# A residual RMSNorm on one core: a small first tile, pieces at the end, and a hardware loop of three tiles per iteration in between

## The chip, the cores and the metric

The kernel runs on 1 core of one Trainium2 chip. The metric is the device time of one execution in microseconds (us), as the median of several executions. All runs were fast (granted clock 1.0). The kernel before ran in every batch on the same chip as what it is compared with; its medians were 3736.6 to 3737.4 us. The batches ran on different chips, so a difference between kernels of two batches carries up to about 1 us of that.

Words used below: SP is the engine that issues all large transfers (DMA) here, DVE the vector engine, ACT the scalar engine. A transfer is *issued* when SP hands it to the DMA queue, *flows* while its packets move (16 side by side, on the core's 16 DMA engines), and has *landed* with the last of its landing records on its semaphore. Each of SP's transfers has 16 such records. A *slot* is a place in on-chip memory.

## The reference

```python
x, residual : 32 x 2048 x 2048 float32;  gamma : 2048 float32;  eps = 1e-6
z   = x + residual
rms = np.sqrt(np.mean(z ** 2, axis=-1, keepdims=True) + eps)
out = (z / rms * gamma).astype(np.float32)
```

That is 65536 rows of 2048 elements: two arrays read, one written, 1610.6 MB in all, and little arithmetic.

## The kernel before

The rows are cut into tiles of 6 x 128 rows (85 of them; a last tile of 2 x 128 is left over). A full tile is 6.29 MB. There are three slots for z, in turn, and one slot for the residual. The parts that matter:

```python
    R = 6
    NZ = 3
    sizes = [R] * n_full + ([left] if left else [])     # 85 full tiles, then one of 2
    ...
    def compute(i):
        # halves of 3 row blocks: DVE adds, ACT squares and sums, ACT takes the root
        ...
        # then DVE: reciprocal, and z * rstd * gamma, row block by row block
        ...

    load_x(0)
    load_r(0)
    load_gamma()
    load_x(1)
    compute(0)
    load_r(1)
    for i in range(1, n_tiles):          # written out by Python, 85 times
        store(i - 1)
        if i + 1 < n_tiles:
            load_x(i + 1)
        compute(i)
        if i + 1 < n_tiles:
            load_r(i + 1)
    store(n_tiles - 1)
```

Waits and semaphores are put in by the framework. In its built program every transfer counts up one of eight DMA semaphores, taken in rotation; in its trace the landing records lie on eight semaphores, 512 to 528 on each.

## Time and profile before

The median is 3736.8 us (3 runs, 3736.49 to 3737.15).

| what | value | how to read it |
|---|---|---|
| DMA queue | 99.7% of 16 engines' span | this is the bound |
| DVE, ACT busy | 62%, 29% | slack of over a third |
| flow in the middle | 433 GB/s | a tile in 43.6 us, three transfers of 14.5 us |
| all bytes at 433.3 GB/s | 3717 us | leaves about 19 us that are not flow |

From the page of the kernel before: busy time of DVE, the totals of the DMA, and the row of the main queue (packets, MB, share of 16 engines).

```profile
DVE 2311.6 (62%) x858; ACT 1078.6 (29%) x1197; POOL 0.2 (0%) x4
...
DMA packets 37180, 1610.83 MB, mean 431 GB/s; under 512 B 4132, under 2 KB 4132, under 8 KB 4132
...
q1 hardware_dynamic: 37152, 1610.63, 99.7%
```

Where are the 19 us? The view of stretches gives, for each stretch of time, its length, the busy time of DVE, ACT and POOL, the granted clock, the share of the DMA and the GB/s moved.

```profile
45.00:50.00 5.00, 3.69 (x3) 4.94 (x7) 0.00 (x0) 1.00 0.65 216
1800.00:1843.60 43.60, 27.04 (x10) 12.61 (x14) 0.00 (x0) 1.00 1.00 433
3690.00:3706.00 16.00, 15.96 (x6) 12.08 (x12) 0.00 (x0) 1.00 0.76 327
3706.00:3712.00 6.00, 5.96 (x5) 0.53 (x3) 0.00 (x0) 1.00 0.10 41
3712.00:3718.00 6.00, 6.00 (x2) 0.00 (x0) 0.00 (x0) 1.00 0.61 262
3718.00:3736.00 18.00, 5.32 (x4) 4.30 (x5) 0.00 (x0) 1.00 0.88 379
```

Two places are not full: one near 46 us, where the second residual load must wait for the adds of a whole first tile (13.1 us in SP's waits), and the last 46 us. In between the queue stays full, and the order of time shows why. This is one tile of the middle, in the kernel before: start, duration, engine (SPq is SP's issuing), line, operation, output and input.

```profile
1825.57 0.33 SPq L66 DMA_DIRECT2D r_slot<-in_residual_dram  x1
...
1839.65 0.34 SPq L69 DMA_DIRECT2D out_dram<-z  x1
1840.04 0.42 SPq L63 DMA_DIRECT2D z<-in_x_dram  x1
1856.11 6.56 DVE L76 TENSOR_TENSOR z<-z,r_slot 128x6144 f32<-128x6144 f32 x1 [16.49 <-DMA r_slot<-in_residual_dram]
```

The residual load is issued at 1825.57 and has landed at 1856.11, when DVE can add it. The store of the previous tile and the next x load go into the queue at 1839.65 and 1840.04, **16 us before that landing**. So when the residual has been moved, 29 us of work (two transfers of 14.5 us) stand behind it. While that backlog lasts, the wait for a landing and the next issue cost no flow (433 GB/s in this stretch). SP's own waits (total, times, longest) show how long it sits idle beside this:

```profile
SPq L66 <- DMA r_slot<-in_residual_dram: 1328.1, 85, 31.4
SPq L69 <- DVE z L98: 1183.3, 86, 20.1
SPq L66 <- DVE rstd L96: 1100.7, 83, 13.3
```

The stores (line 69) wait for DVE's last scaling, never for a residual load.

### The profile page before, as it was taken

What the parts mean: (1) busy time and instruction counts of PE and PEld (TensorE: products, weight loads), DVE (VectorE), ACT (ScalarE), POOL (GpSimd) and SP (SyncE); (2) the same over time, 40 slices, a digit from 0 to 9 for tenths busy, and PEclk for the clock granted to TensorE, in tenths of its full rate; (3) what the DMA queues carried; (4) which work ended last, traced back from release to release, by engine and by line L of the source; (5) the groups of instructions that cost most, each with busy time, mean ns of one, the idle gap of its engine ahead of it and who ended that gap; (6) DMA issues with size and microseconds to landing.
All of it is one profiled execution on the core that took longest, in us unless ns stands there. A gap on an engine that the chain in (4) does not pass through costs nothing.

```text
span 3736.0 us, 2707 instructions
## 1 busy us (share of the span) xinstructions
DVE 2311.6 (62%) x858; ACT 1078.6 (29%) x1197; POOL 0.2 (0%) x4
## 2 busy tenths in 40 slices
DVE  6555666665566666556666655666665566666556
ACT  2222233222223322222332222233222223322223
POOL 0000000000000000000000000000000000000000
DMA  9999999999999999999999999999999999999998
GB/s 410 429 432 434 433 434 432 435 433 434 433 434 433 433 434 434 433 435 432 434 433 434 434 434 433 434 432 435 432 436 432 435 432 435 433 434 433 435 432 369
DMA packets 37180, 1610.83 MB, mean 431 GB/s; under 512 B 4132, under 2 KB 4132, under 8 KB 4132
## 3 DMA queue, kind: packets, MB, share of 16 engines
q1 hardware_dynamic: 37152, 1610.63, 99.7%
q14 instruction: 20, 0.16, 0.0%
q10 hardware_dynamic: 8, 0.03, 0.0%
HBM read 1073.77 MB, written 536.87 MB: 431 GB/s over the span
## 4 chain that ended last, share of the span: by engine, by line
DMA 70%; DVE 30%; issue 0%; ACT 0%; DVEq 0%; SPq 0%
DMA r_slot<-in_residual_dram 70%; DVE z L76 30%; DVE z L98 0%; ACT sq_junk L79 0%; DVE rstd L96 0%; DVEq L160 0%; DVEq L76 0%; SPq L63 0%; ACT rms L86 0%
## 5 line engine op out<-in xcount | busy, mean ns | idle before, releaser
L76 DVE TENSOR_TENSOR z<-z,r_slot 128x6144 f32<-128x6144 f32 x171 | 1111.7, 6542 | 1385.4 <-DMA r_slot<-in_residual_dram 1385.4
L79 ACT ACTIVATE sq_junk<-z 128x2048 f32<-128x2048 f32 x512 | 963.5, 1882 | 2620.0 <-DVE z L76 2603.5
L98 DVE SCALAR_TENSOR_TENSOR z<-z,rstd,gamma_tile 128x2048 f32<-128x2048 f32 x512 | 1173.6, 2347 | 6.0
L79 ACT ACTIVATION_READ_ACCUMULATOR sq_junk<-z 128x1 f32 x512 | 95.5, 186 | 0.0
L86 ACT ACTIVATE rms<-ssq,eps_tile 128x3 f32<-128x3 f32 x171 | 50.7, 296 | 5.5
L96 DVE RECIPROCAL rstd<-rms 128x3 f32<-128x3 f32 x171 | 29.5, 172 | 5.7 <-ACT rms L86 5.7
L114 DVE LOAD_MASK_SELECT gamma_tile<-gamma_tile x1 | 0.0, 14 | 17.8 <-DMA gamma_tile<-in_gamma_dram 17.8
L79 ACT ACT_TABLE_LOAD x1 | 1.3, 1283 | 18.8 <-DMA z<-in_x_dram 18.8
L114 DVE STREAM_SHUFFLE gamma_tile<-gamma_tile 128x2048 f32<-128x2048 f32 x1 | 2.4, 2418 | 0.0
L109 DVE MEMSET gamma_tile<- 128x2048 f32 x1 | 1.8, 1765 | 0.4 <-issue 0.4
L86 ACT ACT_TABLE_LOAD x1 | 1.3, 1283 | 0.0
L60 DVE MEMSET eps_tile<- 128x1 f32 x1 | 0.1, 59 | 0.8 <-PEq L146 0.8
L146 POOL MEMSET const-bfloat16-1.0<- 128x1 bf16 x1 | 0.1, 101 | 0.0
L146 POOL MEMSET const-uint8-127<- 128x1 uint8 x1 | 0.1, 101 | 0.0
L146 POOL MEMSET const-float32-0.0<- 128x1 f32 x1 | 0.1, 98 | 0.2 <-issue 0.2
L146 POOL MEMSET const-float32-1.0<- 128x1 f32 x1 | 0.1, 98 | 0.0
## 6 DMA issues: line engine op xcount, KB each, us to landing
z<-in_x_dram SPq DMA_DIRECT2D x85, 6144.0 KB, 45.0
r_slot<-in_residual_dram SPq DMA_DIRECT2D x85, 6144.0 KB, 30.4
out_dram<-z SPq DMA_DIRECT2D x85, 6144.0 KB, 30.9
z<-in_x_dram SPq DMA_DIRECT2D x1, 2048.0 KB
r_slot<-in_residual_dram SPq DMA_DIRECT2D x1, 2048.0 KB
out_dram<-z SPq DMA_DIRECT2D x1, 2048.0 KB, 7.3
gamma_tile<-in_gamma_dram ACTq DMA_DIRECT2D x4, 8.0 KB
```

The costliest lines, as they stand in the source:

```text
L60: nc.vector.memset(eps_tile, float(eps))
L76: nc.vector.tensor_add(out=z[:, a:b, :], in0=z[:, a:b, :], in1=r_slot[:, a:b, :])
L79: nc.scalar.activation(out=sq_junk, in_=z[:, g, :], func=Act.Square, accum_out=ssq[:, g - a : g - a + 1],)
L86: nc.scalar.activation(out=rms[:, : b - a], in_=ssq[:, : b - a], func=Act.Sqrt, bias=eps_tile, scale=inv_d,)
L96: nc.vector.reciprocal(out=rstd[:, : b - a], in_=rms[:, : b - a])
L98: nc.vector.scalar_tensor_tensor(out=z[:, g, :], in0=z[:, g, :], scalar=rstd[:, g - a : g - a + 1], in1=gamma_tile, op0=mult, op1=mult,)
L109: nc.vector.memset(gamma_tile, 0.0)
L114: nc.vector.stream_shuffle(gamma_tile, gamma_tile, [0] * 32)
L146: nc = _bacc.Bacc("TRN2", target_bir_lowering=False, num_devices=1)
```

## The change

The intent: take away the idle queue at both ends, and shrink the program. The left-over tile of 2 x 128 rows comes first, its residual goes into a z slot that is still free, so that both first and both second loads are issued at once. The last tile, now a full one, is loaded, computed and stored in pieces of two row blocks. The 81 tiles 2 to 82 run in a hardware loop: 27 iterations of three tiles (so that the slots come round), with addresses taken from registers. Its semaphores are not reset at the back edge (its trace has a clear of semaphores only at the end, at line 221); instead the waits compare them with registers that grow each iteration.

```diff
-    sizes = [R] * n_full + ([left] if left else [])
+    sizes = ([left] if left else []) + [R] * n_full
...
+    def pieces(i):
+        k = sizes[i]
+        return [(a, min(a + piece, k)) for a in range(0, k, piece)] if i == last else [(0, k)]
+
+    def r_of(i):
+        return z_slots[NZ - 1] if i == 0 else r_slot
...
+    def cycle(i, at):
+        z_next = z_slots[(i + 1) % NZ]
+        nc.sync.dma_start(out=o_full[at - 1], in_=z_slots[(i - 1) % NZ])
+        nc.sync.dma_start(out=z_next, in_=x_full[at + 1])
+        compute(i)
+        nc.sync.dma_start(out=r_slot, in_=r_full[at + 1])
...
     load_x(1)
+    load_r(1)
     compute(0)
-    load_r(1)
-    for i in range(1, n_tiles):
+    def turn(i):
         store(i - 1)
 ...
-    store(n_tiles - 1)
+    lo = 2
+    n_loop = (last - 1 - lo) // NZ
+    for i in range(1, lo):
+        turn(i)
+    with tc.For_i(0, n_loop * NZ, NZ, iteration_sync="reg_based") as iv:
+        for c in range(NZ):
+            cycle(lo + c, iv + (lo + c - first_full))
+    for i in range(lo + n_loop * NZ, n_tiles):
+        turn(i)
+    store(last)
```

What the diff does not say is in the built program. A body has nine transfers, and the loop has eight DMA semaphores (in the trace of the changed kernel, 864 landing records on the first and 432 on each of the others). Written as a table (S store, L load of x, R load of the residual, in SP's order):

```
transfer   S1 L1 R1 S2 L2 R2 S3 L3 R3
semaphore   0  1  2  3  4  5  6  7  0
```

S1 of iteration j waits for semaphore 0 to hold 32 j counts more than at the start: 16 from the last S1 and 16 from the last R3.

More of the change, by code (lines that the diff above doesn't have):

```diff
@@ L39 @@
     assert n_full * P * R + left * P == n_rows
-    sizes = [R] * n_full + ([left] if left else [])
+    sizes = ([left] if left else []) + [R] * n_full
+    starts = [0]
+    for k in sizes:
+        starts.append(starts[-1] + P * k)
     n_tiles = len(sizes)
@@ L45, in rows @@
         k = sizes[i]
-        a = i * P * R
+        a = starts[i]
         return t[a : a + P * k, :].rearrange("(p r) m -> p r m", r=k)
@@ L51 @@
     slots = ctx.enter_context(tc.tile_pool(name="slots", bufs=1))
-    stats = ctx.enter_context(tc.tile_pool(name="stats", bufs=3))
+    stats = ctx.enter_context(tc.tile_pool(name="stats", bufs=6))
     psum = ctx.enter_context(tc.tile_pool(name="psum", bufs=1, space=bass.MemoryType.PSUM))
@@ L60, with full @@
     nc.vector.memset(eps_tile, float(eps))
+    last = n_tiles - 1
+    piece = 2
+    def pieces(i):
[3 more added lines that the diff above has]
+        return z_slots[NZ - 1] if i == 0 else r_slot
+    first_full = 1 if left else 0
+    def full(t):
+        a = first_full * P * left
+        return t[a:, :].rearrange("(n p r) m -> n p r m", p=P, r=R)
+    x_full, r_full, o_full = full(x_f), full(r_f), full(o_f)
+    def cycle(i, at):
[4 more added lines that the diff above has]
+        nc.sync.dma_start(out=r_slot, in_=r_full[at + 1])
     def load_x(i):
@@ L65, in load_r, with add, square, scale @@
     def load_r(i):
-        nc.sync.dma_start(out=r_slot[:, : sizes[i], :], in_=rows(r_f, i))
+        for a, b in pieces(i):
+            nc.sync.dma_start(out=r_of(i)[:, a:b, :], in_=rows(r_f, i)[:, a:b, :])
     def store(i):
-        nc.sync.dma_start(out=rows(o_f, i), in_=z_slots[i % NZ][:, : sizes[i], :])
-    def compute(i):
-        z = z_slots[i % NZ]
+        for a, b in pieces(i):
+            nc.sync.dma_start(out=rows(o_f, i)[:, a:b, :], in_=z_slots[i % NZ][:, a:b, :])
+    def add(i, a, b):
+        z = z_slots[i % NZ]
+        nc.vector.tensor_add(out=z[:, a:b, :], in0=z[:, a:b, :], in1=r_of(i)[:, a:b, :])
+    def square(i, a, b):
+        n = b - a
+        ssq = stats.tile([P, 3], fp32, name="ssq")
+        for g in range(n):
+            nc.scalar.activation(
+                out=sq_junk,
+                in_=z_slots[i % NZ][:, a + g, :],
+                func=Act.Square,
+                accum_out=ssq[:, g : g + 1],
+            )
+        rms = stats.tile([P, 3], fp32, name="rms")
+        nc.scalar.activation(
+            out=rms[:, :n], in_=ssq[:, :n], func=Act.Sqrt, bias=eps_tile, scale=inv_d
+        )
+        return rms
+    def scale(i, a, b, rms):
+        n = b - a
+        rstd = stats.tile([P, 3], fp32, name="rstd")
+        nc.vector.reciprocal(out=rstd[:, :n], in_=rms[:, :n])
+        for g in range(n):
+            row = z_slots[i % NZ][:, a + g, :]
+            nc.vector.scalar_tensor_tensor(
+                out=row,
+                in0=row,
+                scalar=rstd[:, g : g + 1],
+                in1=gamma_tile,
+                op0=mult,
+                op1=mult,
+            )
+    def compute(i):
+        if i == last:
+            before = None
+            for a, b in pieces(i):
+                add(i, a, b)
+                rms = square(i, a, b)
+                if before is not None:
+                    scale(i, *before)
+                before = (a, b, rms)
+            scale(i, *before)
+            return
         groups = [(a, min(a + 3, sizes[i])) for a in range(0, sizes[i], 3)]
@@ L75, in compute @@
         for a, b in groups:
-            nc.vector.tensor_add(out=z[:, a:b, :], in0=z[:, a:b, :], in1=r_slot[:, a:b, :])
-            ssq = stats.tile([P, 3], fp32, name=f"ssq{a}")
-            for g in range(a, b):
-                nc.scalar.activation(
-                    out=sq_junk,
-                    in_=z[:, g, :],
-                    func=Act.Square,
-                    accum_out=ssq[:, g - a : g - a + 1],
-                )
-            rms = stats.tile([P, 3], fp32, name=f"rms{a}")
-            nc.scalar.activation(
-                out=rms[:, : b - a],
-                in_=ssq[:, : b - a],
-                func=Act.Sqrt,
-                bias=eps_tile,
-                scale=inv_d,
-            )
-            rms_of.append(rms)
-        for (a, b), rms in zip(groups, rms_of):
-            rstd = stats.tile([P, 3], fp32, name=f"rstd{a}")
-            nc.vector.reciprocal(out=rstd[:, : b - a], in_=rms[:, : b - a])
-            for g in range(a, b):
-                nc.vector.scalar_tensor_tensor(
-                    out=z[:, g, :],
-                    in0=z[:, g, :],
-                    scalar=rstd[:, g - a : g - a + 1],
-                    in1=gamma_tile,
-                    op0=mult,
-                    op1=mult,
-                )
+            add(i, a, b)
+            rms_of.append(square(i, a, b))
+        for (a, b), rms in zip(groups, rms_of):
+            scale(i, a, b, rms)
     def load_gamma():
```

## The prediction

> **What bounds it now.** The DMA queue. The page shows 1610.6 MB in 3736.0 us, the queue's packets at 99.7% of 16 engines' span, DVE 62%, ACT 29%. In the middle (stretch 1800 to 1843.6 us) the core moves 433 GB/s; a tile takes 43.6 us, three transfers of 14.5 us. At 433.3 GB/s all bytes take 3717 us, so about 19 us are not flow. Stretches show where: 1.8 us before the first byte; about 4 us up to 93 us (queue empty near 46 to 47.5 us, since the second residual load waits for a full first tile's adds); about 14 us from 3690 us on (laggard DMA engines until 3711, nothing until the store issued at 3714.2, the last landing).
>
> **What the change removes.** With a small first tile whose residual goes into a free slot, the first four loads (16.8 MB, 38.7 us of flow) are queued at once and the first store is ready near 28 us: no gap at the start. With the last tile in pieces the tail's stores queue behind one another; I work out each trigger to fall some 4 us before the queue would run dry. Worth about 15 us: 4 at the start, 11 at the end.
>
> **What it adds.** The branch, register updates and prefetch hint are hidden: [...] SP waits 13 to 31 us for its events in before. The semaphores are not hidden. In the built program the body has nine transfers on eight loop semaphores; the first store of an iteration shares one with the last residual load of the iteration before, and waits for both its earlier counts. So from the second iteration on that store, and the x load behind it in SP's order, wait until this residual load has LANDED. In before, SP issued the store 14 us after that load's issue (1825.57 to 1839.65), 16.5 us before its landing (1856.1); that was the backlog. That load is last in the queue, so the queue drains once per iteration: 26 back edges, plus the loop's exit, where SP waits for every loop transfer and a barrier.
>
> Cost of one drain, estimated from the start of before, where the queue does drain: mean end of flow to mean landing about 1.5 us, mean to last of 16 engines 1.1 us (landing records), wait instructions 0.2 us, issue to flow 1.0 to 1.1 us, plus some for an address from registers: about 4.2 us (3.3 to 5.3). [...] All of it is critical, as DMA is the bound: 26 x 4.2 = 109 us, the exit 5.4 us.
>
> **Sum.** 3717 + 1.8 + 2.9 (last landing) + 109 + 5.4 = 3836 us, 2.7% slower. DVE and ACT have slack and lose nothing.
>
> **What would show it.** SP's waits: a store of line 88 waiting for the residual's DMA, about 16 us, 26 times. Stretches: one hole of about 4 us in DMA per three tiles, period about 135 us against 130.7. Other tiles unchanged at 433 GB/s. No gap at 46 us; no hole like that from 3706 to 3715 in the tail.
>
> **What would make it wrong.** If the shared wait does not drain the queue, 3720 to 3730 us. If a register-addressed transfer issues much slower, or the drain costs under 3.5 us, the sum moves by 26 us per us; under 3.2 us it falls within 2%.

Two passages are cut from this text, since no run of this case shows them: a time for a branch, and a fixed cost of a transfer. No term of the sum is cut: 3717 + 1.8 + 2.9 + 109 + 5.4 = 3836 us stands. That the branch is hidden was the estimate then; its 49 ns (below) and the 31 ns of the prefetch hint were measured afterwards, in the changed kernel. Of the parts of one drain, the first is not what the packets show: for the x load near 46 us they end at 46.43 us in the mean, and the landing records stand at 46.84 us in the mean, 0.4 us later and not 1.5. For an address from registers no number was given; SP issues the x load behind S1 0.62 us after it in the changed kernel (1831.76, 1832.38) and 0.44 us after it without a loop (e3_wait_only: 1829.32, 1829.76). The exit's 5.4 us is an estimate for which the text gives no working.

## The result

| | median us | runs | range |
|---|---|---|---|
| before | 3736.98 | 4 | 3736.49 to 3737.32 |
| changed | 3849.49 | 4 | 3847.14 to 3850.6 |

The ratio is 1.03, with a 95% interval of 1.0283 to 1.0318: slower. (A ratio here is the mean time of one kernel's fast runs over that of the other's of the same rounds, so not quite the ratio of the medians.)

From the page of the changed kernel, the same lines as before:

```profile
DVE 2312.3 (60%) x860; ACT 1075.5 (28%) x1198; POOL 0.2 (0%) x4
...
DMA packets 37737, 1610.67 MB, mean 419 GB/s; under 512 B 4196, under 2 KB 4196, under 8 KB 4196
...
q1 hardware_dynamic: 37728, 1610.63, 98.2%
```

DVE and ACT did the same work in the same time. The queue moved the same bytes, at 419 instead of 431 GB/s over the span. The order of time around a back edge of the changed kernel shows where:

```profile
1801.13 0.33 SPq L91 DMA_DIRECT2D r_slot<-in_residual_dram  x1
...
1831.72 13.03 DVE L106 TENSOR_TENSOR z<-z,r_slot 128x6144 f32<-128x6144 f32 x2 [16.37 <-DMA r_slot<-in_residual_dram]
1831.76 0.36 SPq L88 DMA_DIRECT2D out_dram<-z  x1
1832.38 0.33 SPq L89 DMA_DIRECT2D z<-in_x_dram  x1
```

The residual load of 1801.13 is R3. The store S1 is not issued 14 us after it, as in the kernel before, but at 1831.76, together with the add that this load's landing releases. Nothing stood behind R3 in the queue. The next S1 follows at 1967.17 (same view), so three tiles take 135.41 us here, and 135.2 us in the mean of all iterations but the first; in the kernel before, where two stores at 1839.65 and 1926.81 have one between them, they take 3 x 43.58 = 130.7 us. Stretches of the changed kernel, columns as before:

```profile
45.00:50.00 5.00, 5.00 (x1) 0.00 (x0) 0.00 (x0) 1.00 1.10 469
1829.00:1831.80 2.80, 0.08 (x1) 0.00 (x0) 0.00 (x0) 1.00 0.04 18
1834.00:1967.00 133.00, 78.84 (x30) 37.70 (x42) 0.00 (x0) 1.00 0.98 420
3800.00:3843.00 43.00, 28.60 (x13) 12.90 (x15) 0.00 (x0) 1.00 1.00 429
```

The gap at 46 us is closed and the tail is full, as intended. But for 2.8 us before this S1 the queue is all but empty (18 GB/s), and it is so each time: from the second iteration to the last, S1 lands 17.2 us after R3, where a transfer in full flow takes 14.5 us. SP's waits name the cause, 26 times for 27 iterations, and once for the exit of the loop (line 185):

```profile
SPq L88 <- DMA r_slot<-in_residual_dram: 774.6, 26, 30.3
...
SPq L88 <- DVE z L130: 622.4, 55, 12.8
...
SPq L185 <- DMA r_slot<-in_residual_dram: 29.3, 1, 29.3
```

The mean of 774.6 / 26 = 29.8 us is not all loss: SP begins to wait as soon as it has issued R3, and for the first 14 us it would have waited for DVE anyway.

What the branch takes can be read too. Line 185 of the changed kernel, its instructions on SP's sequencer: count, then duration in ns (least, median, most).

```profile
L185 SPq FUSED_REGOPS  x54: 59/70/73, 59.4 to 3695.5; - x54
...
L185 SPq COMPARE_BRANCH  x28: 44/49/68, 59.2 to 3695.6; - x28
```

Register updates of 70 ns and branches of 49 ns pass while SP would be waiting anyway; whether they cost anything, the second experiment tests.

### The profile page after: what moved, and what is told of

Its sections match the earlier page's. It is cut to its first block, busy times and chain, and to the rows that moved or that the text cites. A ratio compares the mean times of both kernels' runs of the same rounds, so it can differ in the third digit from the quotient of the medians.

```text
span 3848.0 us, 4931 instructions
## 1 busy us (share of the span) xinstructions
DVE 2312.3 (60%) x860; ACT 1075.5 (28%) x1198; POOL 0.2 (0%) x4
## 3 DMA queue, kind: packets, MB, share of 16 engines
q1 hardware_dynamic: 37728, 1610.63, 98.2%
## 5 line engine op out<-in xcount | busy, mean ns | idle before, releaser
L106 DVE TENSOR_TENSOR z<-z,r_slot 128x6144 f32<-128x6144 f32 (+1 forms) x171 | 1107.6, 6517 | 1493.2 <-DMA r_slot<-in_residual_dram 1469.1
L119 ACT ACTIVATE rms<-ssq,eps_tile 128x3 f32<-128x3 f32 (+1 forms) x172 | 51.0, 296 | 5.5
L127 DVE RECIPROCAL rstd<-rms 128x3 f32<-128x3 f32 (+1 forms) x172 | 29.7, 173 | 12.0 <-ACT rms L119 12.0
```

The lines of the kernel that those rows point to most:

```text
L106: nc.vector.tensor_add(out=z[:, a:b, :], in0=z[:, a:b, :], in1=r_of(i)[:, a:b, :])
L119: nc.scalar.activation(out=rms[:, :n], in_=ssq[:, :n], func=Act.Sqrt, bias=eps_tile, scale=inv_d)
L127: nc.vector.reciprocal(out=rstd[:, :n], in_=rms[:, :n])
```

## The experiments

Ten kernels were run, all correct (the labels skip e4). The theory: *the shared semaphore makes one store per iteration wait for a landing, which drains the queue.* The rival R2: *the loop's machinery costs it (back edge, registers, transfers with addresses from registers).* A second rival, R1: *the new start or tail costs it.* (These two names are of rivals and not of the transfers R1 and R2 of the table above; below, a rival is one that misses or falls, a transfer one that lands.)

| label | what it is | median us | range | ratio to before |
|---|---|---|---|---|
| e1_unrolled | no loop, new start and tail | 3728.95 | 3728.7 to 3729.09 | 0.9979 (0.9962 to 0.9995) |
| e2_tenth | loop, a tenth, tiny transfer | 3730.71 | 3730.46 to 3732.14 | 0.9985 (0.9968 to 1.0001) |
| e3_wait_only | no loop, the wait added, 26 times | 3840.37 | 3838.82 to 3840.86 | 1.0276 (1.0259 to 1.0293) |
| e5_six | loop of six tiles | 3732.97 | 3731.71 to 3735.07 | 0.9989 (0.9973 to 1.0006) |
| e6_start_only | no loop, no pieces at the end | 3743.23 | 3743.02 to 3743.74 | 1.0016 (1.0 to 1.0033) |
| e7_split | loop, R3 in halves | 3750.76 | 3748.06 to 3752.84 | 1.0038 (1.0021 to 1.0055) |
| e8_barrier | loop with a barrier per iteration | 3877.86 | 3875.61 to 3878.31 | 1.0375 (1.0357 to 1.0392) |
| e9_wait_each | no loop, the wait added 80 times | 3950.58 | 3949.86 to 3950.68 | 1.057 (1.0553 to 1.0588) |
| e10_wait_second | no loop, the wait added 40 times | 3894.36 | 3893.68 to 3894.88 | 1.042 (1.0403 to 1.0437) |
| e11_split_early | loop, R3 in pieces of 2 and 4 | 3733.86 | 3733.62 to 3733.94 | 0.9991 (0.9974 to 1.0007) |

### The loop written out again

```diff
-    with tc.For_i(0, n_loop * NZ, NZ, iteration_sync="reg_based") as iv:
-        for c in range(NZ):
-            cycle(lo + c, iv + (lo + c - first_full))
+    for i in range(lo, lo + n_loop * NZ):
+        turn(i)
```

> The changed kernel with its hardware loop written out again; small first tile and pieces at the end kept. Theory (the loop's shared semaphore drains the DMA queue 26 times and the exit once, 4.65 us each): all 27 holes go, 3722 to 3727 us; the start and the tail are worth 10 to 15 us against 3737. Rival R1 (start or tail of the change cost time themselves): over 3740. Rival R2 (the loop's own machinery, branch and register-addressed transfers, costs it): also 3722 to 3727, so the next run is to tell them apart.

Measured: 3728.95 us. R1 falls: start and tail together gain 7.6 us (3736.59 to 3728.95), and the loop costs 120.5 us. But the gain is half of what was forecast, and the time lies 2 us above the range. Stretches of this kernel's tail:

```profile
3706.00:3712.00 6.00, 5.96 (x4) 3.85 (x5) 0.00 (x0) 1.00 0.65 279
3712.00:3718.00 6.00, 2.97 (x2) 0.00 (x0) 0.00 (x0) 1.00 1.01 429
3718.00:3727.00 9.00, 0.00 (x0) 0.00 (x0) 0.00 (x0) 1.00 0.38 160
```

The last 9 us move only 160 GB/s. The trace's landing records suggest why: each transfer has 16 of them, read here as one per DMA engine. At 300 us the last of the 16 comes 2.2 us after their mean in the kernel before; at 3670 us 7.3 us after it, and 6 us in this kernel. A few engines fall behind slowly, and at the end the others, done sooner, wait for them. Pieces at the end do not cure that. This is read from the records; no run removed the lag alone.

### The loop kept, the sharing moved

```diff
         compute(i)
+        if i == lo + NZ - 1:
+            nc.sync.dma_start(out=pad_tile, in_=gamma.partition_broadcast(1)[:, :4])
         nc.sync.dma_start(out=r_slot, in_=r_full[at + 1])
```

> The loop, its branch, register addresses and barrier at the exit all kept; one 16-byte load is put into the body before its last residual load, so that ten transfers go round the eight semaphores. The first store of an iteration then shares its semaphore with the tiny load, and the residual's wait moves to the x load behind that store. Theory: the store is queued 14 us ahead again, the 26 holes vanish, only the exit's 5 us stay: 3727 to 3733 us. Rival R2 (branch, register updates, register-addressed issue): unchanged, 3845 to 3855 us.

Measured: 3730.71 us; three tiles of the middle again flow at full rate (stretch of this kernel), and SP's waits changed places:

```profile
1800.00:1930.80 130.80, 81.32 (x31) 37.71 (x42) 0.00 (x0) 1.00 1.00 433
```

```profile
SPq L89 <- DMA pad_tile<-in_gamma_dram: 396.1, 26, 15.3
SPq L90 <- DMA r_slot<-in_residual_dram: 354.5, 26, 13.8
```

The store (here line 89) now waits for the tiny load, the x load (line 90) for the residual, with a 14.5 us store ahead of it in the queue. Branch, registers, register addresses and the exit's barrier are all still there. R2 falls: 16 bytes per iteration gave back (3849.49 - 3730.71) / 26 = 4.57 us each, and what is left of the loop costs 1.8 us in all (3730.71 - 3728.95). This is also the cleanest measure of one drain, since both kernels have the exit.

### No loop, the wait alone

```diff
     for i in range(lo, lo + n_loop * NZ):
+        if i > lo and (i - lo) % NZ == 0:
+            for k in (i - 1, i + 1):
+                bit = z_slots[k % NZ][:1, R - 1, :4]
+                nc.vector.scalar_tensor_tensor(
+                    out=bit, in0=r_slot[:1, 0, :4], scalar=0.0, in1=bit, op0=mult,
+                    op1=mybir.AluOpType.add,
+                )
         turn(i)
```

The two operations add 0 times a residual value to four elements of the slot that is to be stored and of the slot that is to be loaded. So DVE waits for the residual, and store and x load wait for DVE.

> No loop; the written-out kernel, where every third store and the x load behind it are made to wait for the landing of the next tile's residual, by two 4-element VectorE operations that read the residual's slot and leave the values as they are, 26 times. Theory: the wait alone costs what the loop did, 26 times 4.6 us over the written-out kernel: 3842 to 3852 us. Rival R2: the waits cost nothing, 3722 to 3730 us.

Measured: 3840.37 us, 111.4 us over the same kernel without the waits, 4.3 us for each. The waits of SP in this kernel show the copied wait:

```profile
SPq L102 <- DVE z L189: 792.2, 26, 31.3
```

The wait without a loop costs 111.4 us of the loop's 120.5 us (2 us below the range; 4.3 us instead of 4.57, and the 0.3 us between them is not explained). The loop without the wait costs 1.8 us. Together these two runs settle the cause.

### Six tiles per iteration

```diff
-    n_loop = (last - 1 - lo) // NZ
+    NB = 2 * NZ
+    n_loop = (last - 1 - lo) // NB
 ...
-    with tc.For_i(0, n_loop * NZ, NZ, iteration_sync="reg_based") as iv:
-        for c in range(NZ):
+    with tc.For_i(0, n_loop * NB, NB, iteration_sync="reg_based") as iv:
+        for c in range(NB):
```

> The loop with six tiles in its body, 13 iterations, 18 transfers on eight semaphores. The first store now waits for the last x load's landing, only about 2 us after it is ready, with a residual load of 14.5 us still queued behind that; the x load waits for the residual. Theory: no holes although the loop goes round, only the exit's 5 us: 3727 to 3735 us. Rival R2 (a cost per back edge): 13 of 27 costs stay, about 3785 us.

Measured: 3732.97 us. With 18 transfers, S1 shares its semaphore with the last x load and L1 with the last residual load, and no drain is left: SP waits 12 times for each of these two loads (14.9 and 13.8 us in the mean), and the stretch from 1800 to 1930.8 us flows at 433 GB/s. It is not the longer body that helped, but which transfer meets which: 13 iterations at a cost per back edge would have kept 12 or 13 costs.

### The tail without pieces

In the written-out kernel the last tile is treated as any other.

```diff
-        return [(a, min(a + piece, k)) for a in range(0, k, piece)] if i == last else [(0, k)]
+        return [(a, min(a + piece, k)) for a in range(0, k, piece)] if False else [(0, k)]
 ...
-        if i == last:
+        if False:
```

> No loop; the small first tile kept, the pieces at the end undone: the last, full tile is loaded, computed and stored whole. The first 93 us moved 12 to 17 GB/s more with the small first tile, worth 2.6 to 3.7 us; without pieces the last full tile's residual must land, 27 us of compute pass, and a 14.5 us store follow with nothing beside it: some 12 to 18 us more than the written-out kernel with pieces (3729), so 3741 to 3747 us, slower than before. If the pieces are worth nothing, 3729.

Measured: 3743.23 us, as expected. Between 3712 and 3718 us the queue moves nothing, while DVE works on the last tile:

```profile
3712.00:3718.00 6.00, 5.96 (x5) 4.33 (x6) 0.00 (x0) 1.00 0.00 0
```

So moving the small tile to the front needs the pieces: without them it is 6 us slower than before, with them 7.6 us faster.

### The last residual load in two pieces

```diff
         compute(i)
-        nc.sync.dma_start(out=r_slot, in_=r_full[at + 1])
+        for a in (0, 3) if i == lo + NZ - 1 else (0,):
+            b = a + 3 if i == lo + NZ - 1 else R
+            nc.sync.dma_start(out=r_slot[:, a:b, :], in_=r_full[at + 1][:, a:b, :])
```

> The loop of three tiles; only the body's last residual load is issued in two halves, so that again ten transfers go round eight semaphores, all of them real ones. The first store of an iteration waits for the first half's landing (7.3 us of the second half still queued), the x load behind it for the second half. Theory: the store is queued before the queue is empty, so 3729 to 3735 us. Rival R2: 3845 to 3855 us.

Measured: 3750.76 us: 98.7 us better than the changed kernel, so R2 misses again, but 16 us above the theory's range, about 0.8 us per iteration over the written-out kernel. The queue had not been thought of as 16 engines. The landing records of this run have the slowest engine 3 to 3.5 us behind the mean and about 5 us behind the first; the store waits for the slowest, and by then the fastest are nearly through the 7.3 us of the second half. That this is the cost was a guess.

To test this, the pieces were made two and four row blocks, so that 9.7 us stand behind the first:

```diff
+        for a, b in ((0, 2), (2, R)) if i == lo + NZ - 1 else ((0, R),):
```

> The three-tile loop with the last residual load of the body in pieces of two and four rows instead of three and three (the halves gave 3750.8 where 3729 to 3735 was expected). If what was missed there is that the store waits for the slowest of the 16 engines, 3 us behind the mean, while the others run through the 7.3 us that are left, then the longer second piece (9.7 us) leaves time enough: 3730 to 3738 us. If the split itself or the loop costs it, about 3750 again.

Measured: 3733.86 us, in the range. So the split as such was not the cost, and a larger margin for the slowest engine took it away. How a short margin makes the loss is not shown: by the landing records of the run with halves, the store itself still landed 14.5 us after the transfer before it, and the loss fell on the residual load R1, two transfers later (15.0 us in the mean, against 14.5 us with pieces of two and four).

### A barrier at each back edge

```diff
-    with tc.For_i(0, n_loop * NZ, NZ, iteration_sync="reg_based") as iv:
+    with tc.For_i(0, n_loop * NZ, NZ, iteration_sync="barrier") as iv:
```

> The changed kernel with the loop's other kind of synchronisation, a barrier of all engines and a reset of the semaphores at each back edge. Theory: the queue drains 26 times as in the changed kernel, for the same 4.65 us, and the barrier and reset come on top, since the store waits for them: at the changed kernel's exit a store followed the last landing 0.85 us later than inside the loop, so 1 to 2.5 us more for each of 26: 3875 to 3915 us.

Measured: 3877.86 us, (3877.86 - 3849.49) / 26 = 1.1 us per back edge more than the changed kernel. SP waits at the back edge (line 185) 27 times for the residual's landing, 812.6 us, and 52 times for TensorE's queue, 9.0 us. The kind of synchronisation chosen by the change saved this 1.1 us and not the 4.6 us of the drain: as the transfers were numbered, its one wait was nearly as strict as the barrier.

### How large is one drain?

The same added wait before every tile, and before every second tile.

```diff
-        if i > lo and (i - lo) % NZ == 0:
+        if i > lo:
```

> No loop; the added wait of the earlier run (store and x load wait until the next residual has landed) put before every tile from the fourth on, 80 times instead of 26. If each drain costs the same, 4.3 us as measured with 26 of them (3840.4 less 3729.0): 3729 plus 80 times 4.3, 4060 to 4085 us. If drains cost less when they come often (engines start each time in step), under 4050.

Measured: 3950.58 us, (3950.58 - 3728.95) / 80 = 2.8 us each: the expected 4.3 us failed, and the other forecast, a lower cost when drains come often (under 4050 us), held. The stores in the order of time of this run stand 46.27 us apart, 2.7 us more than a tile of before:

```profile
1837.49 0.34 SPq L102 DMA_DIRECT2D out_dram<-z  x1
...
1883.76 0.34 SPq L102 DMA_DIRECT2D out_dram<-z  x1
```

So a drain is dearer here when more transfers follow it: 2.8 us with three from one drain to the next, 4.3 us with nine (e3_wait_only). The steps between full landings of successive transfers, worked out from the landing records, show where (in us, means over all drains between 100 and 3600 us; 14.5 is a transfer in full flow):

```
                          S1     L1     R1     S2     L2     R2     S3     L3     R3
e9, wait each tile       17.2   14.6   14.6   (drain)
e10, each second tile    17.2   14.6   15.7   14.7   14.7   14.5   (drain)
changed kernel           17.2   14.6   15.6   14.7   14.7   14.8   14.6   14.7   14.5
e1, no drain             14.5 throughout
```

The hole is 17.2 - 14.5 = 2.7 us in all of them. After a drain all engines start in step (the 16 landings lie within 0.4 to 0.8 us, against 5.2 us in the written-out kernel), and then the transfer before a change from loading to storing (R1) lands about 1.1 us late, the next few a little late. With a wait before every tile, that change comes only behind the next hole, and nothing of this is seen. The run with 40 waits was made to test it:

```diff
+        if i > lo and (i - lo) % 2 == 0:
```

> No loop; the added wait before every second tile, 40 times. With 26 of them one drain came to 4.3 us, with 80 to 2.8 us. Theory T1 (the empty queue itself costs 2.7 us, and the 16 engines, set in step by it, lose 0.8 to 1 us more at the next change from a load to a store, then less until they are out of step): such a change comes once between two drains here, so 3.5 to 3.8 us each, 3869 to 3881 us. If a drain has one fixed cost and only its count was misread: 2.8 us each gives 3841, 4.3 us each gives 3901.

Measured: 3894.36 us, (3894.36 - 3728.95) / 40 = 4.1 us each. None of the three forecasts held. It excludes a fixed 2.8 us, and it lies 13 us above T1's range and only 7 us below the fixed 4.3 us (3901), which the run with 80 waits had excluded. So a drain does cost more when more transfers follow it, as T1 has it, but the loss after the hole is 1.4 us by this difference, not 0.8 to 1.1. That the loss needs engines in step is not shown: the loop with halves lost 0.5 us at the same place, R1, with its 16 landings 4.8 us apart. What makes it stays open.

## Why the prediction was right or wrong

1. **The bound: right.** DMA at 99.7% before and 98.2% after; DVE and ACT busy times equal within 1%.
2. **The mechanism: right, and shown.** The store waits for the landing of R3, 26 times, the queue is empty for 2.8 us, the period is 135.2 us in the mean (forecast 135). The tenth transfer takes the cost away with the loop in place; the bare wait brings it back without a loop.
3. **One drain: mis-sized.** Forecast 4.2 us, measured 4.57 us ((3849.49 - 3730.71) / 26), so 119 us instead of 109. Its make-up was also off: the hole between full landings is 2.7 us, less than the sum of latencies suggested, and some 1.9 us (4.57 less 2.7) come after it, in the transfers that follow, which the forecast did not know of and whose cause stays open.
4. **"No hole in the tail", worth 11 us: the step that failed.** The prediction read "laggard DMA engines until 3711" in the profile and then counted their time as recoverable. The first 93 us move 423 GB/s instead of 406 (stretches), which at 433 GB/s is worth (423 - 406) x 93 / 433 = 3.7 us, as forecast (4). Start and tail together are worth only 7.6 us in the written-out kernel, so about 4 us are left for the tail. What the runs show in its place: the slowest engine stays 6 us behind the mean and ends last, so the time of the laggards is not recovered. In the changed kernel itself this hardly shows, since its drains bring the engines together: its last transfer's landings lie within 1.2 us.
5. **Branch and registers hidden: right.** They take 49 and 70 ns; kernels with the loop and without the drain (3730.7, 3733.0, 3733.9) lie within 5 us of the written-out one.
6. **SP's wait "about 16 us": misread.** It is 29.8 us, since it starts at R3's issue; the 16 us are only the part beyond DVE's finish.
7. **The sum.** 3836 forecast, 3849.5 measured. Of the 13.5 us, 9.6 are the drains (26 x 0.37) and the other 3.9 the start, tail and exit. In these, two misses partly cancel, which was luck: the kernel without the loop was forecast at 3717 + 1.8 + 2.9 = 3721.7 us and took 7.3 us more, while what the loop costs beside its drains, forecast at 5.4 us for the exit, came to 1.8 us.

The fastest version found is the written-out kernel with the new start and tail: 3728.95 us, 0.2% better than before. The loop can be had for 2 us more (with the tiny transfer) or 5 us more (pieces of two and four).

## What to carry to other kernels

In this kernel, bound by DMA (99.7%), what had to be kept was the backlog in the queue: running it empty cost 2.8 to 4.6 us each time. In one like it, ask of every wait on the issuing engine how many microseconds of transfers still stand in the queue when it ends, counted for the slowest of the 16 engines (9.7 us were enough here; with 7.3 us about 0.8 us per iteration was lost). When transfers go into a hardware loop, count them against the semaphores they go round (nine on eight cost 4.57 us per iteration here). If the body's last transfer shares one with the next iteration's first, split or add a transfer, or unroll once more, so that the sharing falls where something is queued behind: the three ways left 1.8 us (one transfer added), 4.0 us (six tiles) and 4.9 us (pieces of two and four) over the written-out kernel. Do not count the time of lagging engines at the end of a trace as a gain from a new order of stores: here it did not come.
